# One block of a diffusion backbone: modulation sums ordered behind weight splits, norms by halves, TensorE repeats products while it waits

## The chip, the cores and the metric

One core of a Trainium2 chip runs the whole program. The metric is the device time of one execution in microseconds; below it, "span" is the part of one profiled execution that the trace covers. An instruction queue belongs to each engine: TensorE (PE, with its weight loads as PEld), VectorE (DVE), ScalarE (ACT), GpSimd (POOL), and SyncE (SP), which issues the weight transfers. Each engine works its queue in order and waits on semaphores of the others.

## The reference

For 256 latent tokens and 256 context tokens of width 2048, in float32:

```python
mod_l = jnp.split(silu_c @ w_mod[l] + b_mod[l], 6, axis=-1)
mod_c = jnp.split(silu_cc @ w_mod[l] + b_mod[l], 6, axis=-1)
hl = modulate(rms_norm(xl, norm1_g[l]), mod_l[0], mod_l[1])
hc = modulate(rms_norm(xc, norm1_g[l]), mod_c[0], mod_c[1])
zl = hl @ w_in[l] + b_in[l]               # conv a1, a2 | gelu u, v | q | k | v | three gates
...
y_conv = silu(layer_norm(depthwise_conv31(a1 * sigmoid(a2)))) @ w_conv_out
y_sgu = spatial_gating(gelu(uv)) @ w_sgu_out
y_att = attention_2d(q, k, v, kc, vc) @ w_na_out
x1 = xl + mod_l[2] * ((g_conv * y_conv + g_sgu * y_sgu + g_att * y_att) @ w_o + b_o)
h2 = modulate(rms_norm(x1, norm2_g[l]), mod_l[3], mod_l[4])
x2 = x1 + mod_l[5] * (square(relu(h2 @ w_ff1 + b1)) @ w_ff2 + b2)
out = rms_norm(x2, final_g)
```

The last seven lines are cut to their sense.

## The kernel before, in words

**Products.** Every large product is taken in two parts: an operand is split into a high part that the fast float32 form of TensorE holds exactly, and the rest. A weight piece is 128 rows by 1024 numbers, 512 KB. `Stream` (`fetch`, L71 to L91) brings each in by one transfer on SP into `raw` (eight buffers), ScalarE casts it into `whi` (L90), VectorE subtracts to get `wlo` (L91); `whi` and `wlo` have four buffers each. `mm_w` (L172, L173) takes the weights as stationary operand and writes a "pair", one matmul over 512 and one over 256 columns; `mm_x` (L178 to L180) takes the tokens as stationary operand and writes three matmuls over 512 columns.

**Steps.** The program is one list of steps, `st.steps`. A step is a number of pieces and a function that uses them. `Stream.run` goes through the list and fetches and splits four pieces ahead (`AHEAD`). So the list sets the order on every engine: a split stands on VectorE where its piece is fetched, ahead of the step four pieces earlier. `gate` and `open` hold back pieces until a point in the program, so that their splits don't stand ahead of something urgent.

**Stages of the span.** 0 to 30 us: opening (modulation of the first two rows of tiles by matmuls with 32 columns, norm 1, hidden states h). 30 to 262: k and v of both token sets, in five row blocks, each with its own modulation (`mod_block`, `post`: a reduction `gv` at L335, then transposes of the tokens, `hT` at L348, then h). 263 to 345: q, with attention begun (scores `S` at L532 and L533, maxima `mx` at L534 and L536). To 544: the conv inputs a1 and a2, u and v with GELU. 544 to 956: three branches, n = 0, 1, 2, with their gates. 956 to 1047: w_o. 1047 to 1054: norm 2. To 1768: feed-forward. To 1777: the final norm.

**Modulation, the other four chapters** (`mod_cols`, `modq`). 16 sums, four chapters by four column blocks, in 128 steps of one unsplit 512 KB piece each. VectorE sums up the rows times the condition, two instructions a step (`ga`, L878 and L880). At the end of a sum TensorE takes part: four transposes (`mcol`, L909) or two products with ones (`mrow`, L899). Steps are put between product steps by `MODS_KV`, `MODS_Q`, `MODS_G`: two after every step of the last row blocks once the early modulation is through, one after every q step, two in three steps of the branches n = 1 and 2; the last 32 steps in the feed-forward.

**Conv norm** (`convq`). One entry after each step of branch 1: sums, mean, eight variance steps, `conv_rstd` (L671 to L674, TensorE, VectorE, POOL), `conv_spread` (L699, L700: a diagonal of the row factors times ones, `crs`), eight `conv_out`.

**Norm 2** (`norm2`, `h2_make`). The square sums of both token halves, one reduction, scaling, power on POOL, a spread by two diagonals, then the first four tiles of h2. `x1_transpose` (L1054) turns the residual by tiles: of block 0 to 2 among the products of w_o, of block 3 behind the spread.

## Time and profile before

| | us |
|---|---|
| median of three runs | 1774.8 (1773.57 to 1776.71) |
| the profiled execution | 1779.37 |
| its span | 1777.5 |
| TensorE busy in it | 1729.2 |
| VectorE busy | 1329.9 |
| ScalarE busy | 862.6 |
| mean granted TensorE clock | 0.993 |

A row of a timeline gives the start, the length, the engine, the line of the code, what is written from what, the shapes and how many instructions were joined; in brackets stand the idle time just before it and what ended that. A granted clock of 1.00 is 2.4 GHz, 0.50 is 1.2 GHz. Lengths of matmuls overlap, since they are pipelined; the distance of two starts is what one costs. The page's share of busy time is a mean over stages with different limits, so each place is read in its own stretch.

### The profile page before, as it was taken

The numbers are of one execution on the slowest core, as the hardware profiler recorded it, in microseconds if no ns is written. First come the engines' busy times: TensorE is split into PE (matmuls) and PEld (weight loads), VectorE is DVE, ScalarE is ACT, GpSimd is POOL, SyncE is SP. The second block draws the span as 40 slices with busy tenths as digits, with TensorE's granted clock in tenths as the row PEclk, the third lists the DMA queues.
The fourth block names the chain that finished last, engine by engine and source line by source line (L and its number), as shares of the span: only waits on it lengthen the run. The fifth ranks groups of instructions, "written<-read, shape, count | busy, mean of one in ns | idle before, by whom it ended". The sixth has DMA issues, their size and how long they took to land.

```text
span 1777.5 us, 24004 instructions
## 1 busy us (share of the span) xinstructions
PE 1729.2 (97%) x8727; PEld 1420.9 (80%) x8727; DVE 1329.9 (75%) x2098; ACT 862.6 (49%) x1290; POOL 134.1 (8%) x174
## 2 busy tenths in 40 slices
PE   6999998999999999999999999999999999999997
PEld 3667787788888888778878878888888888888886
DVE  4656999799999977999877569756775576656665
ACT  4433335987555344644444455533543354334443
POOL 2221340111000100200000010000000000000000
PEclk9999999999999999999999999999999999999999
DMA  9887788656766668899995568757876775666552
GB/s 323 274 307 271 257 260 262 162 145 185 221 189 198 181 211 291 285 332 331 320 338 194 188 192 267 239 194 246 257 251 196 241 220 191 204 193 189 186 193 83
DMA packets 266968, 411.86 MB, mean 232 GB/s; under 512 B 13182, under 2 KB 128050, under 8 KB 266850
## 3 DMA queue, kind: packets, MB, share of 16 engines
q1 hardware_dynamic: 259410, 391.21, 68.1%
q0 software_dynamic: 6864, 18.07, 3.8%
q8 instruction: 68, 1.11, 0.3%
q10 hardware_dynamic: 576, 1.05, 0.2%
q14 instruction: 50, 0.41, 0.1%
HBM read 408.18 MB, written 2.10 MB: 231 GB/s over the span
## 4 chain that ended last, share of the span: by engine, by line
PE 70%; issue 10%; DVE 9%; DMA 7%; ACT 2%; SPq 1%; POOL 0%; DVEq 0%; POOLq 0%; ACTq 0%
PE bk L172 17%; PE bk L178 11%; PE bk L180 11%; PE bk L179 11%; PE bk L173 9%; DMA raw<-in_w_mod_dram 6%; DVE wlo L91 4%; DVE ga L880 3%; PE k L172 2%; PE gemv L313 1%; DMA raw<-in_w_in_dram 1%; PE k L173 1%; PE vb L178 1%; PE vb L180 1%; PE vb L179 1%
## 5 line engine op out<-in xcount | busy, mean ns | idle before, releaser
L90 ACT CAST whi<-raw 128x1024 fp32r<-128x1024 f32 x544 | 570.3, 1050 | 612.0 <-PE bk L180 389.6
L91 DVE TENSOR_TENSOR wlo<-raw,whi 128x1024 fp32r<-128x1024 f32 x544 | 668.3, 1231 | 256.5 <-ACT whi L90 254.2
L172 PE MATMUL bk<-h,whi 128*128 128x512 f32 x1536 | 545.5, 399 | 0.2 <-DVE vN L406 0.2
L173 PE MATMUL bk<-h,wlo 128*128 128x256 f32 x1536 | 431.4, 281 | 2.1 <-DVE wlo L91 2.1
L172 PEld LDWEIGHTS bk<-h,whi 128*128 128x128 f32 x1536 | 289.6, 189 | 72.5 <-issue 3.1
L173 PEld LDWEIGHTS bk<-h,wlo 128*128 128x128 f32 x1536 | 291.3, 190 | 4.7 <-DVE wlo L91 3.6
L880 DVE SCALAR_TENSOR_TENSOR ga<-raw,cst,ga 128x512 f32<-128x512 f32 x240 | 185.4, 774 | 65.2 <-DMA raw<-in_w_mod_dram 62.3
L180 PE MATMUL bk<-whi,g 128*128 128x512 f32 x512 | 199.2, 389 | 0.0
L179 PE MATMUL bk<-wlo,g 128*128 128x512 f32 x512 | 199.2, 389 | 0.0
L178 PE MATMUL bk<-whi,g 128*128 128x512 f32 x512 | 199.2, 389 | 0.0
L179 PE MATMUL bk<-wlo,h 128*128 128x512 f32 x448 | 175.2, 391 | 1.9 <-DVE wlo L91 1.9
L178 PE MATMUL bk<-whi,h 128*128 128x512 f32 x448 | 176.2, 393 | 0.0
L180 PE MATMUL bk<-whi,h 128*128 128x512 f32 x448 | 175.1, 391 | 0.0
L180 PEld LDWEIGHTS bk<-whi,g 128*128 128x128 f32 x512 | 96.1, 188 | 20.0
L178 PEld LDWEIGHTS bk<-whi,g 128*128 128x128 f32 x512 | 96.1, 188 | 20.0
L179 PEld LDWEIGHTS bk<-wlo,g 128*128 128x128 f32 x512 | 96.1, 188 | 19.8
L641 DVE SCALAR_TENSOR_TENSOR cT<-uT,wcT,cT 128x244 f32<-128x244 f32 (+14 forms) x240 | 105.0, 479 | 0.5
L179 PEld LDWEIGHTS bk<-wlo,h 128*128 128x128 f32 x448 | 84.6, 189 | 20.4 <-DVE wlo L91 3.2
L180 PEld LDWEIGHTS bk<-whi,h 128*128 128x128 f32 x448 | 84.4, 188 | 17.8
L178 PEld LDWEIGHTS bk<-whi,h 128*128 128x128 f32 x448 | 84.5, 189 | 17.2
L172 PE MATMUL k<-h,whi 128*128 128x512 f32 x256 | 93.9, 408 | 3.2 <-DVE h L358 2.8
L173 PE MATMUL k<-h,wlo 128*128 128x256 f32 x256 | 72.0, 283 | 0.8 <-DVE wlo L91 0.8
(268 smaller groups left out, 2048.4 us busy)
## 6 DMA issues: line engine op xcount, KB each, us to landing
raw<-in_w_ff_dram SPq DMA_DIRECT2D x256, 512.0 KB, 4.1
raw<-in_w_in_dram SPq DMA_DIRECT2D x208, 512.0 KB, 4.5
raw<-in_w_mod_dram SPq DMA_DIRECT2D x192, 512.0 KB, 5.0
raw<-in_w_o_dram SPq DMA_DIRECT2D x32, 512.0 KB, 3.9
raw<-in_w_na_out_dram SPq DMA_DIRECT2D x16, 512.0 KB, 4.2
raw<-in_w_sgu_out_dram SPq DMA_DIRECT2D x16, 512.0 KB, 5.4
raw<-in_w_conv_out_dram SPq DMA_DIRECT2D x16, 512.0 KB, 6.8
bias<-in_na_rpb_dram POOLq DMA_DIRECT2D x16, 192.0 KB, 5.5
```

The costliest lines, as they stand in the source:

```text
L90: nc.scalar.copy(hv, rv)
L91: nc.vector.tensor_tensor(lv, rv, hv.bitcast(F32), ALU.subtract)
L172: PE.matmul(bk, lhsT=hi[:, j, c0 : c0 + P], rhs=xhl, start=start, stop=False)
L173: PE.matmul(bk[:, T:], lhsT=lo[:, j, c0 : c0 + P], rhs=xhl[:, :T], start=False, stop=stop)
L178: PE.matmul(bk, lhsT=xh, rhs=hi, start=start, stop=False)
L179: PE.matmul(bk, lhsT=xh, rhs=lo, start=False, stop=False)
L180: PE.matmul(bk, lhsT=xl, rhs=hi, start=False, stop=stop)
L313: PE.matmul(gb[j][32 * q : 32 * q + 32, :cols], lhsT=cst[:, g], rhs=raw[:, r], start=g < 4, stop=g >= NK - 4, tile_position=(0, 32 * q))
L641: V.scalar_tensor_tensor(a[:, lo:hi], u[:, lo + d : hi + d], wj, a[:, lo:hi], ALU.mult, ALU.add)
L880: V.scalar_tensor_tensor(a[0], raw[:, r], sc, a[0], ALU.mult, ALU.add)
```

## The change

Nothing that is computed changes. The order and the place of work do:

- Opening: seven of the eight pieces of the first modulation block are multiplied a second time into a spare bank (`warm`), and twelve transposes follow the first `hT`; late parameters are loaded in the middle of the block; only one weight split may stand ahead of the first h (`FIRST`).
- A modulation step's sums are issued behind the split of up to two later pieces (`behind`, `LAG`); that sets the order on VectorE's queue and adds no semaphore.
- Modulation steps are placed anew: in the k/v blocks in the last block alone (12 steps, 25 before), 12 of 16 in q, 8, 24 and 20 in the three branches (0, 32 and 32 before), 20 in w_o, 32 in the feed-forward as before. Chapter 4 comes first, 3 third.
- Conv norm: empty entries between its steps, conv outputs at every second step. Residual loads and bias rows (`xb_load`) of three blocks go into branch 2.
- GELU: one VectorE instruction less per tile.
- Norm 2: by token halves, the first while the products of the second run; the third block's `x1_transpose` and 22 transposes (`refill`) behind the last product, 8 more behind the spread; epsilon is a fifth column of the square sums.
- End: the last block is multiplied with the final gain ahead of the row factor.

```diff
 RBUF = 8
-MODS_Q = 1
-MODS_G = 3
+MODS_Q = (0, 1, 2)
+MODS_G = ((2, 8), (0, 2, 4, 6, 8, 10), (0, 3, 5, 8, 10))
+MODS_O = 20
 TAPS_C, TAPS_S, TAPS_G = 1, 3, 3
 AHEAD = 4
+LAG = 2
...
-        nc.vector.tensor_tensor(lv, rv, hv.bitcast(F32), ALU.subtract)
+        self.low[j] = nc.vector.tensor_tensor(lv, rv, hv.bitcast(F32), ALU.subtract)
...
+            self.at = used
             used += len(pieces)
             self.more = lambda used=used: more(used + AHEAD)
             fn(*mine)
+    def behind(self):
+        later = [j for j in self.low if self.at < j <= self.at + LAG]
+        return self.low[max(later)] if later else None
...
+                if bi == 0 and (j, r0) != (1, NK - rt):
+                    for r in range(rt):
+                        q = (r0 + r) % 4
+                        PE.matmul(warm()[32 * q : 32 * q + 32, :cols], lhsT=cst[:, r0 + r], rhs=raw[:, r],
+                                  start=True, stop=True, tile_position=(0, 32 * q))
...
+            if bi == 0 and vs == (0,):
+                for i in range(12):
+                    PE.transpose(warm()[:, :P], gb["ge"][:, :P], ident)
...
-    convq = [lambda i=i: conv_sum(i) for i in (0, 2, 3, 4, 5, 6, 7)] + [conv_mean] + [lambda i=i: conv_var(i) for i in range(8)] + [conv_rstd, conv_spread] + [lambda i=i: conv_out(i) for i in range(8)]
...
+    convq = [lambda i=i: conv_sum(i) for i in (0, 2, 3, 4, 5, 6, 7)] + [idle, conv_mean] + [lambda i=i: conv_var(i) for i in range(8)] + [idle, conv_rstd, idle, idle, conv_spread, idle] + [f for i in range(8) for f in (lambda i=i: conv_out(i), idle)]
...
-        V.tensor_tensor(q, q, z, ALU.mult)
+        S.activation(q, z, AF.Square, scale=GC0 ** 0.5)
+        V.scalar_tensor_tensor(q, q, 1.0, z, ALU.add, ALU.mult)
...
         def mk(r0):
             def fn(raw):
+                split = st.behind()
                 for r in range(2):
...
-                        V.tensor_scalar(a[0], raw[:, r], sc, None, ALU.mult)
-                    else:
-                        V.scalar_tensor_tensor(a[0], raw[:, r], sc, a[0], ALU.mult, ALU.add)
+                    with tc.issue_after(split.ins) if split else nullcontext():
+                        if r0 + r == 0:
+                            V.tensor_scalar(a[0], raw[:, r], sc, None, ALU.mult)
+                        else:
+                            V.scalar_tensor_tensor(a[0], raw[:, r], sc, a[0], ALU.mult, ALU.add)
...
-    for ch in (3, 4, 2, 5):
+    for ch in (4, 2, 3, 5):
...
-    st.steps += early[: ends[0]]
-    st.do(lambda: posts[0]((0,)))
+    st.steps += early[: ends[0] // 2]
     st.do(late_params)
+    st.steps += early[ends[0] // 2 : ends[0]]
+    if FIRST:
+        st.gate(FIRST)
+    def opening():
+        posts[0]((0,))
+        if FIRST:
+            with tc.issue_after(last["h"].ins), tc.issue_after(last["hi"].ins):
+                st.open()
+    st.do(opening)
...
-            if sent >= len(early):
+            if bi == len(BLOCKS) - 1:
                 mod_steps(MODS_KV)
...
-            mod_steps(MODS_Q)
+            mod_steps(i in MODS_Q)
...
+            with tc.issue_after(gload[2, min(cb + 1, 3)].ins):
+                GP.dma_start(xb[cb], x[0][:, cb * 512 : (cb + 1) * 512].rearrange("(t p) n -> p t n", p=P))
...
-                if n and i % MODS_G and len(modq) > 32:
+                if i in MODS_G[n] and len(modq) > 32 + MODS_O:
                     mod_steps(1)
+                if n == 2 and cb and i == XB:
+                    st.do(xb_load(cb - 1))
...
-    while len(modq) > 32:
-        mod_steps(1)
...
-    for cb in range(4):
-        st.do(xb_load(cb))
...
+    st.do(xb_load(3))
...
             st.steps.append(s)
+            if i % 4 and len(modq) > 32:
+                mod_steps(1)
             if cb == 0 and i == 0:
                 st.do(lambda: m_split(3))
-            if cb and i == 1:
+            if cb in (1, 2) and i == 1:
                 st.do(lambda cb=cb: x1_transpose(cb - 1))
...
+    def refill(n):
+        if "fill" not in n2:
+            n2["fill"] = aux("fill")
+        for _ in range(n):
+            PE.transpose(n2["fill"][:, :P], xb[3][:, 0, :P], ident)
+    def norm2(t):
+        if t == 0:
+            n2["rb"] = aux("n2")[:, :T]
+        rs = tp.tile([P, 1], F32, tag="rs", bufs=2, name=nm("n2rs"))
+        V.tensor_reduce(rs, ss2[:, t], axis=AX.X, op=ALU.add)
+        GP.tensor_tensor(rs, rs, mhalf[:, :1], ALU.pow)
+        dg = tp.tile([P, P], F32, tag="dg", bufs=2, name=nm("dg"))
+        V.tensor_scalar(dg, ident, rs, None, ALU.mult)
+        if t:
+            with tc.issue_after(last["mm"].ins):
+                x1_transpose(2, n2["sq"])
+                refill(22)
+        mm = PE.matmul(n2["rb"][:, t * P : (t + 1) * P], lhsT=ones, rhs=dg, start=True, stop=True)
+        h2_make(0, t * P, (t + 1) * P)
+        if t:
+            with tc.issue_after(mm.ins):
+                refill(8)
...
+            V.tensor_tensor(f, xa[kt // 4][:, kt % 4, a:b], n2["rb"][:, a:b], ALU.mult)
+            n2["high"] = S.activation(d[:, a:b], f, AF.Identity, bias=m2B[:, kt : kt + 1])
+            n2["last"] = V.scalar_tensor_tensor(d[:, T + a : T + b], f, m2B[:, kt : kt + 1], d[:, a:b].bitcast(F32), ALU.add, ALU.subtract)
...
+        end = tmp(512, "end")
+        V.tensor_tensor(end, d, fg[3], ALU.mult)
...
-        V.tensor_scalar(rs, rs, 1.0 / D, EPS, ALU.mult, ALU.add)
...
-        with tc.issue_after(n2["last"].ins):
+        with tc.issue_after(n2["last"].ins), tc.issue_after(n2["high"].ins):
...
-    for n in (2, 4, 6):
+    for n in (1, 4, 6):
         st.gate(n)
-    st.do(norm2)
+    st.do(lambda: norm2(0))
+    st.do(lambda: norm2(1))
```

Three places in the order of the queues. The number behind a name is that of its buffer; x2 means twice in a row. First, VectorE at the end of the fourth k/v block, before the change (`ga` modulation sums, `vN` evictions of v, `gv` and `m1B` the modulation of the next block, for which TensorE's transposes `hT` wait):

```order
L880 SCALAR_TENSOR_TENSOR ga_2135<-raw_2075,cst,ga_2135 128x512
L406 TENSOR_TENSOR vN_554<-vN_554,vb_1934 128x512
L880 SCALAR_TENSOR_TENSOR ga_2135<-raw_2075,cst,ga_2135 128x512
L880 SCALAR_TENSOR_TENSOR ga_2135<-raw_2133,cst,ga_2135 128x512
L91 TENSOR_TENSOR wlo_2072<-raw_2069,whi_2071 128x1024
L406 TENSOR_TENSOR vN_563<-vN_563,vb_1948 128x512
L335 TENSOR_REDUCE gv_1982<-gp_1985 128x8
L335 TENSOR_REDUCE gv_1982<-gp_1993 128x8
L338 TENSOR_TENSOR m1B<-gv_1982,pa_104 128x4 x2
```

The same place after it:

```order
L419 TENSOR_TENSOR t_1916<-k_1907,t_1916 128x256
L437 TENSOR_TENSOR vN_436<-vN_436,vb_1928 128x512
L437 TENSOR_TENSOR vN_445<-vN_445,vb_1942 128x512
L437 TENSOR_TENSOR vN_597<-vN_597,vb_1956 128x512
L97 TENSOR_TENSOR wlo_1923<-raw_1920,whi_1922 128x1024
L437 TENSOR_TENSOR vN_606<-vN_606,vb_1970 128x512
L365 TENSOR_REDUCE gv_1984<-gp_1987 128x8
L365 TENSOR_REDUCE gv_1984<-gp_1995 128x8
L369 TENSOR_TENSOR m1B<-gv_1984,pa_104 128x4 x2
```

The sums are gone from here; the reduction `gv` stands behind evictions and one split.

Second, VectorE in branch 2 at the end of its second column block (`m` the merged branches, `wlo` weight splits), before the change:

```order
L847 TENSOR_TENSOR m_6096<-m_6096,th_8349 128x512
L880 SCALAR_TENSOR_TENSOR ga_8579<-raw_8582,cst,ga_8579 128x512
L91 TENSOR_TENSOR wlo_8489<-raw_8486,whi_8488 128x1024
L880 SCALAR_TENSOR_TENSOR ga_8579<-raw_8582,cst,ga_8579 128x512
L880 SCALAR_TENSOR_TENSOR ga_8579<-raw_8604,cst,ga_8579 128x512
L91 TENSOR_TENSOR wlo_8527<-raw_8524,whi_8526 128x1024
L880 SCALAR_TENSOR_TENSOR ga_8579<-raw_8604,cst,ga_8579 128x512
L91 TENSOR_TENSOR wlo_8558<-raw_8555,whi_8557 128x1024
```

The same place after it:

```order
L881 TENSOR_TENSOR m_6073<-m_6073,th_8284 128x512
L97 TENSOR_TENSOR wlo_8379<-raw_8376,whi_8378 128x1024
L917 SCALAR_TENSOR_TENSOR ga_8309<-raw_8330,cst,ga_8309 128x512
L97 TENSOR_TENSOR wlo_8403<-raw_8400,whi_8402 128x1024
L917 SCALAR_TENSOR_TENSOR ga_8309<-raw_8330,cst,ga_8309 128x512
L97 TENSOR_TENSOR wlo_8421<-raw_8418,whi_8420 128x1024
L917 SCALAR_TENSOR_TENSOR ga_8309<-raw_8396,cst,ga_8309 128x512 x2
L97 TENSOR_TENSOR wlo_8469<-raw_8466,whi_8468 128x1024
```

Each sum stood directly ahead of a split; now a sum of `raw_8330` stands behind the splits of `raw_8376` and `raw_8400`, which were fetched later.

Third, TensorE at norm 2 (`bk` the last product of w_o, `n` the spread of the row factors, `x1T` the transposed residual), before the change:

```order
L180 MATMUL bk_9550<-whi_9616,mhl_9068 128x512
L700 MATMUL n_890_9704<-dg_9705,ones_r 128x128
L700 MATMUL n_890_9704<-dg_9708,ones_r 128x128
L1054 MATMUL x1T_9870<-ident,xb_9028 128x128 x4
L1054 MATMUL x1T_9877<-ident,xb_9028 128x128 x4
L172 MATMUL bk_9759<-h_893_9711,whi_9634 128x512
L173 MATMUL bk_9759<-h_893_9711,wlo_9635 128x256
```

The same place after it:

```order
L194 MATMUL bk_9553<-whi_9632,mhl_8973 128x512
L1143 MATMUL n_888_9710<-dg_9714,ones_r 128x128
L1105 MATMUL x1T_9741<-ident,xb_8820 128x128 x4
L1105 MATMUL x1T_9748<-ident,xb_8820 128x128 x4
L1128 MATMUL fill_9755<-ident,xb_8937 128x128 x22
L1143 MATMUL n_888_9710<-dg_9738,ones_r 128x128
L1128 MATMUL fill_9755<-ident,xb_8937 128x128 x8
L1105 MATMUL x1T_9950<-ident,xb_8937 128x128 x4
L1105 MATMUL x1T_9957<-ident,xb_8937 128x128
L184 MATMUL bk_9839<-h_891_9717,whi_9650 128x512
L185 MATMUL bk_9839<-h_891_9717,wlo_9651 128x256
```

One half of the spread stands before the change's fillers and one behind; the third block's transposes and 30 others stand in the gap; of the last block's eight, five come ahead of the first product.

## Rows read from the trace of the kernel before

**Rows 1.** The page: busy time of TensorE, and the group of modulation sums.

```profile
PE 1729.2 (97%) x8727; PEld 1420.9 (80%) x8727; DVE 1329.9 (75%) x2098; ACT 862.6 (49%) x1290; POOL 134.1 (8%) x174
...
L880 DVE SCALAR_TENSOR_TENSOR ga<-raw,cst,ga 128x512 f32<-128x512 f32 x240 | 185.4, 774 | 65.2 <-DMA raw<-in_w_mod_dram 62.3
```

**Rows 2.** Waits of TensorE: what waited, for what; us in total, times, longest.

```profile
PE n L700 <- DVE dg L699: 3.9, 1, 3.9
PE S L532 <- DVE mx L536: 3.6, 2, 3.2
...
PE bk L179 <- DVE wlo L91: 2.5, 4, 1.2
PE bk L173 <- DVE wlo L91: 2.1, 3, 1.5
PE mcol L909 <- DVE ga L880: 2.0, 1, 2.0
PE S L533 <- ACT kl L501: 1.6, 2, 1.3
```

**Rows 3.** Stretches: length, busy PE, PEld, DVE, ACT, POOL, granted clock, DMA, GB/s.

```profile
203.70:207.10 3.40, 3.40 (x10) 2.66 (x9) 3.37 (x10) 1.93 (x4) 0.00 (x0) 0.50 1.05 358
...
560.00:580.00 20.00, 20.00 (x90) 16.54 (x89) 20.00 (x27) 9.25 (x10) 0.91 (x2) 1.00 0.71 214
...
1050.20:1057.10 6.90, 6.02 (x22) 5.30 (x23) 5.33 (x14) 2.62 (x6) 5.18 (x10) 0.51 0.73 219
```

**Rows 4.** Timeline of TensorE in the opening, and one later modulation piece.

```profile
14.96 3.98 PE L313 MATMUL gemv<-raw,cst 128*32 128x256 f32 x32
...
23.90 1.08 PE L313 MATMUL gemv<-raw,cst 128*32 128x256 f32 x8 [0.42 <-DMA raw<-in_w_mod_dram]
...
29.99 0.77 PE L172 MATMUL k<-h,whi 128*128 128x512 f32 x1 [2.79 <-DVE h L358]
...
31.41 0.63 PE L172 MATMUL k<-h,whi 128*128 128x512 f32 x1
...
33.57 0.39 PE L172 MATMUL k<-h,whi 128*128 128x512 f32 x1
...
33.92 0.39 PE L172 MATMUL k<-h,whi 128*128 128x512 f32 x1
...
62.72 1.07 PE L313 MATMUL gemv<-raw,cst 128*32 128x512 f32 x8
```

**Rows 5.** Timeline at the fourth k/v block's end, and VectorE as attention starts.

```profile
199.59 1.53 DVE L880 SCALAR_TENSOR_TENSOR ga<-raw,cst,ga 128x512 f32<-128x512 f32 x2
...
203.01 0.91 PE L348 MATMUL hT<-ident,nat 128*128 128x128 f32 x6 [2.75 <-DVE gv L335]
...
288.62 1.54 DVE L880 SCALAR_TENSOR_TENSOR ga<-raw,cst,ga 128x512 f32<-128x512 f32 x2
```

**Rows 6.** Timeline of TensorE in branch 1, at the conv norm.

```profile
731.08 0.50 PE L671 MATMUL cvar<-ones_r,cq 128*128 128x1 f32 x4
...
735.95 0.73 PE L700 MATMUL crs<-dg,ones_r 128*128 128x128 f32 x4 [1.48 <-DVE dg L699]
```

**Rows 7.** Timeline in branch 2: a sum that waits, and TensorE behind it.

```profile
896.46 0.75 DVE L880 SCALAR_TENSOR_TENSOR ga<-raw,cst,ga 128x512 f32<-128x512 f32 x1 [5.20 <-DMA raw<-in_w_mod_dram]
...
898.41 0.50 PE L179 MATMUL bk<-wlo,h 128*128 128x512 f32 x1 [1.20 <-DVE wlo L91]
```

**Rows 8.** Timeline of w_o's transposes at full clock, then of norm 2.

```profile
984.47 1.04 PE L1054 MATMUL x1T<-ident,xb 128*128 128x128 f32 x8
...
1047.25 0.69 DVE L1043 TENSOR_TENSOR t<-bk,mrow 128x512 f32<-128x512 f32 x1 [0.21 <-PE bk L180]
...
1052.06 1.92 PE L1054 MATMUL x1T<-ident,xb 128*128 128x128 f32 x8
1053.85 0.80 PE L172 MATMUL bk<-h,whi 128*128 128x512 f32 x1
```

**Rows 9.** Timeline of VectorE at the end.

```profile
1770.46 0.15 DVE L1139 TENSOR_SCALAR n3rs<-n3rs 128x1 f32<-128x1 f32 x1
```

More of the change, by code (lines that the diff above doesn't have):

```diff
@@ L1 @@
-from contextlib import ExitStack
+from contextlib import ExitStack, nullcontext
 import concourse.bass as bass
@@ L66, in __init__ @@
         self.n = 0
+        self.at = 0
+        self.low = {}
     def add(self, pieces, fn):
@@ L173, in mm_w @@
         PE.matmul(bk[:, T:], lhsT=lo[:, j, c0 : c0 + P], rhs=xhl[:, :T], start=False, stop=stop)
+    last = {}
     def mm_x(bk, xhl, t, hi, lo, start, stop):
@@ L179, in mm_x @@
         PE.matmul(bk, lhsT=xh, rhs=lo, start=False, stop=False)
-        PE.matmul(bk, lhsT=xl, rhs=hi, start=False, stop=stop)
+        last["mm"] = PE.matmul(bk, lhsT=xl, rhs=hi, start=False, stop=stop)
     w_mod, b_mod, w_in, b_in = w_mod[0], b_mod[0], w_in[0], b_in[0]
@@ L298, in tile_block, with warm @@
         S.copy(vbias[:, i * 512 : (i + 1) * 512], vps)
+    spare = []
+    def warm():
+        if not spare:
+            spare.append(bank("warm"))
+        return spare[0]
     def mod_block(bi):
@@ L820, in tile_block @@
     gbias = {}
+    gload = {}
     def gate_bias(br, cb):
@@ L998, in tile_block, with xb_load, fn @@
     att_steps(100)
+    xb = [None] * 4
+    xa = [None] * 4
+    ss2 = cp.tile([P, 2, 5], F32, name="ss2")
+    GP.memset(ss2[:, :, 4:], EPS)
+    def xb_load(cb):
+        def fn():
+            xb[cb] = unit([P, 2, 512], name="xb")
+            with tc.issue_after(gload[2, min(cb + 1, 3)].ins):
+                GP.dma_start(xb[cb], x[0][:, cb * 512 : (cb + 1) * 512].rearrange("(t p) n -> p t n", p=P))
+            bo = tmp(512, "bo")
+            with tc.issue_after(gload[2, min(cb + 1, 3)].ins):
+                GP.dma_start(bo, bcast(b_o[0][cb * 512 : (cb + 1) * 512], P))
+            V.tensor_tensor(bo, bo, mrow[2, cb], ALU.mult)
+            for t in range(2):
+                V.tensor_tensor(xb[cb][:, t], xb[cb][:, t], bo, ALU.add)
+        return fn
     branches = [(2, w_na_out[0], lambda kt: oT[kt][:, kt % 2]), (1, w_sgu_out[0], lambda kt: sgT[kt][:, kt % 2]),
@@ L1014, in tile_block @@
                     st.do(convq.pop(0))
[L1015 removed]
+                if i in MODS_G[n] and len(modq) > 32 + MODS_O:
                     mod_steps(1)
+                if n == 2 and cb and i == XB:
+                    st.do(xb_load(cb - 1))
         if n == 0:
             taps_steps(1000)
[L1020 to L1037 removed]
+    n2 = {}
     def o_done(cb):
@@ L1044, in fn, with x1_transpose @@
             V.tensor_tensor(d, d, f, ALU.add)
-            S.activation(f, d, AF.Square, accum_out=ss2[:, t, cb : cb + 1])
+            n2["sq"] = S.activation(f, d, AF.Square, scale=D ** -0.5, accum_out=ss2[:, t, cb : cb + 1])
         return fn
-    def x1_transpose(cb):
+    def x1_transpose(cb, after=None):
         xa[cb] = unit([P, 4, T], name="xa")
@@ L1054, in x1_transpose @@
                     PE.transpose(b2[:, i * T + tt * P : i * T + (tt + 1) * P], xb[cb][:, tt, (kk + i) * P : (kk + i + 1) * P], ident)
-            for i in range(2):
-                kt = 4 * cb + kk + i
-                S.activation(xa[cb][:, kk + i], b2[:, i * T : (i + 1) * T], AF.Copy, scale=m2A[:, kt : kt + 1])
-    for cb in range(4):
-        st.do(xb_load(cb))
+            with tc.issue_after(after.ins) if after else nullcontext():
+                for i in range(2):
+                    kt = 4 * cb + kk + i
+                    S.activation(xa[cb][:, kk + i], b2[:, i * T : (i + 1) * T], AF.Copy, scale=m2A[:, kt : kt + 1])
+    st.do(xb_load(3))
     for cb in range(4):
@@ L1091, in tile_block @@
     gT = [None] * NK
     ac = [None] * 4
-    ss3 = cp.tile([P, 2, 4], F32, name="ss3")
+    ss3 = cp.tile([P, 2, 5], F32, name="ss3")
+    GP.memset(ss3[:, :, 4:], EPS)
     NB = DFF // D
```

59 lines of the change are left out of this document (18 added, 41 removed).

## Prediction

> **What bounds the kernel now.** I read the page's table of busy time first. TensorE is busy for 1729.2 of the 1777.5 us of the span, VectorE for 75%, ScalarE for less [rows 1]. So the time is TensorE's, and only two things can be won: the 48 us in which it stands still, and the stretches in which its clock is halved. The waits by engine come second. Before the first weight product nothing can be gained in large sums (inputs arrive). After it, each line names a place and what ended the wait: norm 2 (3.9), the scores at the start of attention (3.6 and 1.6), products that wait for a weight piece's low part (2.5 and 2.1), a column of the modulation (2.0) [rows 2]. Third come stretches with the granted clock: after a standstill of 2 to 4 us the clock stands at 0.50, which is 1.2 GHz, for 3.40 us, and the engine is full all that time [rows 3]. At half speed 3.40 us do the work of 1.70, so each such standstill costs 1.7 us more than its wait. Three are alike, from 203.7, 299.3 and 760.1; the fourth, at norm 2, is 1050.2 to 1057.1. Fourth, the timeline of VectorE at each place shows why it was late: it works its queue in order, and a modulation sum (774 ns [rows 1]) that waits for its transfer holds up the weight split or the score behind it. From 560 to 580 VectorE is full and TensorE waits for nothing [rows 3]: there the engines are level, and VectorE has no room.
>
> **The change part by part.** All against the profiled run of 1779.4 us.
>
> *(a) Opening.* Before, the eight pieces of the first modulation block run at half speed: eight matmuls with 256 columns take 1.08 us, as eight with 512 columns do later [rows 4]; TensorE rests between pieces and again for 2.79 us before the first product at 29.99, and the products still take 0.63 at 31.41 and 0.39 at 33.57, a pair of them then 0.35 from start to start [rows 4]. The records hold no clock there; by the products it changes at 33.06. Half of 33.06 − 29.99 is 1.5 us. The change repeats seven of the eight pieces and adds twelve transposes, so that the engine has no pause; if the clock is full by 29.99, that is 1.5. A copy of parameters and two small scalings leave VectorE's path to the first product: at no less than 0.15 each, as a scaling at the end [rows 9], some 0.5. Together +2.0. Other end: if the clock stays at half, a piece costs 0.86 (two groups of four, 0.43 apart), and 15 times 0.86 from 14.96 ends at 27.9, where the last piece now ends near 24.8: 3.1 later, and 0.4 for transfers that wait for buffers which the repeats hold, −3.5. I take **+2.0**, since the engine would run without a gap from 14.96, and the products from 29.99 on show that a run without a gap brings the clock up.
>
> *(b) End of the k/v blocks.* The reduction that the hidden states need stood behind modulation sums (two in a row at 199.59, three before them); TensorE waited 2.75 [rows 5] and then ran its 3.40 us at half speed [rows 3], 1.70: 4.45 in all. Now modulation stands in the last row block alone, and the order of VectorE has no sum ahead of that reduction in any block but the last. What is late next is the reduction's own chain, some tenths. **+4.2**, ends 0 and 4.5.
>
> *(c) Start of attention.* The waits are 3.2 and 0.4, then 1.3 [rows 2], with one half-speed stretch of 1.70: 6.6. The first maxima stood behind five sums from 288.62 on [rows 5] and two splits, 5 × 0.774 + 2 × 1.23 = 6.3. Now one step less stands in each group of four, and between the evictions and the maxima there is one split and no sum. From the eviction to the freed bank that leaves some 4.7 us of VectorE's work, where the 16 product pairs in between give 16 × 0.35 = 5.6. But VectorE must have caught up by then. **+4.5**, ends −1 and +7.3 (all of it, and the small waits from 333 to 345 too).
>
> *(d) Conv norm.* From the sum of squares on TensorE to its spread lie 731.08 to 735.95, and TensorE waited 1.48 of that [rows 6]; 12 products stood between, 36 stand there now, 8.0 us at 0.22 each (90 instructions in 20.00 [rows 3]), where 4.9 are needed. The column that came too late at 757 (2.0 [rows 2]) and the 1.70 that followed it stood behind the rows of the conv output, which now come at every second step. **+5.0**, ends 1.5 and 5.2.
>
> *(e) Splits behind waiting sums.* At 896 a sum waited 5.20 us for its transfer; the split behind it came late, and TensorE waited 1.20 [rows 7]. All such places are 2.5 and 2.1 [rows 2]. Now a step's sums stand behind the splits of up to two later pieces, so a split waits for its own piece alone. What pays for it: a raw buffer is held for longer, so SP's next transfer starts later, and what is queued behind a waiting sum is now the third split. **+4.2**, ends 0 and 4.6.
>
> *(f) Norm 2.* From the last product's end at 1047.25 to the first product at 1053.85 the chain is eviction 0.69, residual, square, reduction, scaling, power, spread, eight transposes, h [rows 8]. By halves, the first half is worked off while 24 products of the second run, so only one half stands behind the last product; one scaling is gone (0.15 as [rows 9], 0.2 with its gap), and one of two diagonals with its spread product leaves the path (between the power and the transposes at 1052.06; I estimate 0.4): 0.6 earlier. The third block's eight transposes, which stood among the products of the last block, take 1.04 at full clock [rows 8] and delay the products by 0.87 (0.11 from start to start); they go into the gap. Of the fourth block's, three move behind the first products, −0.3. 22 and 8 more transposes fill the gap; if they hold the clock, the half speed from 1053.85 to 1057.1, 3.2 us, costs 1.6 less. In all 0.6 + 0.87 − 0.3 + 1.6 = 2.8, of which I take **+2.6**. Other end: fillers that run at half speed (1.92 for eight [rows 8], so 5.3 for 22 and 7.2 with the eight ahead) end at 1054.4 and hold up the spread by 3, less what is gained: −1.5. Upper end 3.4.
> Here a rule speaks against the change. The trace shows transposes at half speed at 1052.06, but behind a standstill, so it cannot tell what they do to the clock. The Trainium skill, "TensorE: Matmul & The Clock Gate", Part 4 (PE-mode transpose), says that transposes don't count as TensorE activity in the same way. By it the fillers would not keep the clock; by the rows alone I can't say.
>
> *(g) End.* The path loses one scaling (0.15 and its gap, 0.24 from 1770.46 to the power [rows 9]), and the last multiplication loses an operand: **+0.4**, ends 0.2 and 0.5. The GELU loses one VectorE instruction for each of twelve tiles (of at most 0.69 [rows 8], the smaller ones half as wide; estimated at 3.8 in all), which TensorE doesn't wait for.
>
> *(h) New waits.* Sixteen sums of modulation (four chapters by four column blocks), each finished by a product on TensorE, now come later on VectorE against the splits. The order gives the lead, the splits that VectorE has done ahead of the sum beyond the one that TensorE last used: before it was −5 to −1 at thirteen places, and +2 at three; now it is +1 to +3 at all sixteen. Of the three with +2, two waited for nothing and one for 2.0 [rows 2], and no place with a negative lead waited. So a wait at each is from 0 to 2.0, 0 to 32 in all. A split takes 1.23, the products of a piece 2.7 (12 at 0.22) or 2.8 (eight pairs), so VectorE gains on TensorE with every piece. I take **−3**, nearer to the two that were free, since the conv rows that stood ahead of the third are spaced now.
>
> Sum: 2.0 + 4.2 + 4.5 + 5.0 + 4.2 + 2.6 + 0.4 − 3 = 19.9. The profiled run would take 1759.5. The median of the runs is 4.6 under that run, so 1774.8 − 19.9 = **1755** (rounded).
>
> **The rivals.**
> R1, slower: the sixteen finishing products wait. Mechanism: a sum put behind two later splits ends only when those pieces have come and been split; TensorE, in order, stands at the product (place: the branches and the feed-forward). At 2.0 each [rows 2] it is 32 instead of 3: 1774.8 − 22.9 + 32 = 1784. It is slower from 22.9 / 16 = 1.4 us a place. For it: the 2.0 at lead +2. Against it: two other such places were free.
> R2: VectorE is full from 420 to 640, and eight steps with 16 sums go into the first branch there, 16 × 0.774 = 12.4, less 3.8 for the GELU: 8.6 that TensorE may have to pay. 1755 + 8.6 = 1763.5. For it: 20.00 of 20.00 [rows 3]. Against it: TensorE waits for nothing there, so a reserve of unknown size is left.
> R3: the repeats of the opening don't bring the clock up. Four pieces ran in a row from 14.96 to 18.94, and a piece at 23.90 was still at half speed [rows 4], which speaks for it; that the pieces have pauses between them speaks against it. 2.0 becomes −3.5: 1760.5.
> R4: the transposes of norm 2 don't keep the clock. 1.6 and a little more of (f) is missing: 1757. The rule cited in (f) would give this.
> R5: the change doesn't do what it says, as each wait has a second cause just behind it (VectorE's whole load of sums stays the same, and each is only moved): within 0.2% of 1774.8.
>
> **How the numbers follow.** The forecast's case, 1748 to 1759, has 0.40, R4 lying within it at near half of that. R3 alone 0.22, R2 alone 0.14, both together, near 1769, 0.06. R5 0.06, R1 0.08, better than 1748 0.04. A difference under 0.2% (3.5 us) can't be told from none by a measurement of this kernel. Faster by more: 0.40 + 0.22 + 0.14 + 0.06 + 0.04 = 0.86; within 0.06; slower 0.08. For 8 in 10 the range reaches from below the forecast's case to R2 and R3 together: 1746 to 1771.
>
> **What would show it.** (a): pairs at 0.35 from the first k product on, which stands before 29.5; R3: 0.64, and a later one. (b), (c): no wait for gv or for mx over 0.5 us, and no clock of 0.50 near 204 or 299. (d): no wait of crs; mcol under 0.5. (e): the lines of waits for wlo under 1 us. (f): granted clock 1.0 from 1048 to 1057, less the shift; R4: 0.5 at the first feed-forward products. (h), R1: lines mcol and mrow in the waits, their sum and count. R2: products waiting for wlo or banks between 420 and 680, with VectorE full. The forecast is wrong if TensorE's waits after the opening are still over 15 us in all, or a new line stands at their head.

## The result, and the profile after

| | before | after |
|---|---|---|
| median of four runs, us | 1775.76 (1773.57 to 1780.57) | 1758.07 (1755.90 to 1758.92) |
| ratio, 95% interval | | 0.9875 (0.9856 to 0.9895) |
| profiled execution, us | 1779.37 | 1758.92 |
| its span | 1777.5 | 1757.1 |

The forecast was 1755, in a range of 1746 to 1771. By the medians the change is worth 17.7 us, by the two spans 20.4, since the profiled execution of before was one of its longer ones. Steps are weighed below by the spans, as the sum was.

The page of after, against [rows 1]: busy time of the engines; the share of the chain that ended last, by engine; and the groups of weight splits and of modulation sums (busy us, mean ns, then idle time just before them).

```profile
PE 1729.2 (98%) x8825; PEld 1423.0 (81%) x8825; DVE 1331.4 (76%) x2094; ACT 866.7 (49%) x1294; POOL 130.9 (7%) x177
...
PE 79%; ACT 1%; issue 1%; DVE 1%; POOL 0%; POOLq 0%; DVEq 0%; ACTq 0%
...
L97 DVE TENSOR_TENSOR wlo<-raw,whi 128x1024 fp32r<-128x1024 f32 x544 | 669.3, 1232 | 289.2 <-ACT whi L96 282.4
...
L917 DVE SCALAR_TENSOR_TENSOR ga<-raw,cst,ga 128x512 f32<-128x512 f32 x240 | 183.6, 765 | 2.3
```

TensorE's busy time is the same 1729.2 us to a tenth, although 98 instructions were added; what was saved is time in which it stood still. The last row says how. VectorE stood idle for 65.2 us just ahead of modulation sums, 62.3 of it for their transfers [rows 1]; now it is 2.3. The sums take as long as before, but when one comes to the head of the queue its piece has landed.

The waits of TensorE, against [rows 2] (us in total, times, longest):

```profile
...
PE k L184 <- DVE h L389: 2.2, 2, 2.0
PE k L184 <- DVE t L419: 1.0, 1, 1.0
PE hT L379 <- ACT nat L275: 0.9, 1, 0.9
PE S L564 <- ACT kl L532: 0.9, 1, 0.9
PE mcol L946 <- DVE ga L917: 0.8, 1, 0.8
...
PE mrow L936 <- DVE ah L934: 0.5, 1, 0.5
```

The lines for n, for mx, for wlo and for crs are gone, and nothing new over 1.0 has come. Where the time went is read from the start of the first product of each stage in the two traces:

| start of | before | after | shift |
|---|---|---|---|
| first k product | 29.99 | 30.19 | +0.2 |
| first q product | 262.86 | 260.72 | −2.1 |
| first product with attention's output (branch 0) | 565.47 | 556.74 | −8.7 |
| first of branch 1's second part | 700.21 | 691.43 | −8.8 |
| first of branch 2's second part | 839.70 | 826.21 | −13.5 |
| first of w_o | 956.35 | 939.11 | −17.2 |
| last of w_o | 1046.83 | 1030.13 | −16.7 |
| first of the feed-forward | 1053.85 | 1035.85 | −18.0 |
| last product | 1767.64 | 1747.40 | −20.2 |
| end of the span | 1777.5 | 1757.1 | −20.4 |

The opening of after, against [rows 4], and its granted clock (length, busy PE, PEld, DVE, ACT, POOL, clock, DMA, GB/s):

```profile
18.48 1.08 PE L335 MATMUL gemv<-raw,cst 128*32 128x256 f32 x8
...
24.85 0.61 PE L335 MATMUL gemv<-raw,cst 128*32 128x256 f32 x8
...
30.19 0.47 PE L184 MATMUL k<-h,whi 128*128 128x512 f32 x1 [2.05 <-DVE h L389]
...
31.49 0.63 PE L184 MATMUL k<-h,whi 128*128 128x512 f32 x1
```

```profile
31.08:34.49 3.41, 3.41 (x13) 2.83 (x12) 2.66 (x5) 2.03 (x5) 0.00 (x0) 0.50 1.05 382
```

The pieces run twice as fast from about 21 on, so the clock came up with the repeats, which before it hadn't (that it needs them isn't shown, see a1). But TensorE rested 2.05 us before the first product, the clock fell at 31.08 after all, and the first product came 0.2 later than before.

Norm 2 of after, against [rows 8]:

```profile
1031.45 2.56 PE L1128 MATMUL fill<-ident,xb 128*128 128x128 f32 x22
...
1034.06 0.49 PE L1143 MATMUL n<-dg,ones_r 128*128 128x128 f32 x2
1034.39 1.04 PE L1128 MATMUL fill<-ident,xb 128*128 128x128 f32 x8
...
1035.26 0.71 PE L1105 MATMUL x1T<-ident,xb 128*128 128x128 f32 x5
...
1035.85 0.50 PE L184 MATMUL bk<-h,whi 128*128 128x512 f32 x1
```

The fillers run at full speed, 0.11 us each, and the first products do too.

### The profile page after: what moved, and what is told of

Read it like the earlier page. It is cut to its first block, busy times and chain, and to the rows that moved or that the text cites. A ratio compares the mean times of both kernels' runs of the same rounds, so it can differ in the third digit from the quotient of the medians.

```text
span 1757.1 us, 24169 instructions
## 1 busy us (share of the span) xinstructions
PE 1729.2 (98%) x8825; PEld 1423.0 (81%) x8825; DVE 1331.4 (76%) x2094; ACT 866.7 (49%) x1294; POOL 130.9 (7%) x177
## 4 chain that ended last, share of the span: by engine, by line
PE 79%; ACT 1%; issue 1%; DVE 1%; POOL 0%; POOLq 0%; DVEq 0%; ACTq 0%
PE bk L184 18%; PE bk L194 16%; PE bk L193 16%; PE bk L192 16%; PE bk L185 9%; PE o L597 1%; PE pT L586 1%; ACT whi L96 0%; PE mrow L936 0%; PE S L563 0%; PE S L564 0%; PE mix L842 0%; PE mT L891 0%; PE mcol L946 0%; ACT s L570 0%
## 5 line engine op out<-in xcount | busy, mean ns | idle before, releaser
L672 DVE SCALAR_TENSOR_TENSOR cT<-uT,wcT,cT 128x248 f32<-128x248 f32 (+14 forms) x240 | 104.6, 481 | 0.5
L193 PEld LDWEIGHTS bk<-wlo,h 128*128 128x128 f32 x448 | 84.1, 188 | 17.2
```

The costliest lines, as they stand in the source:

```text
L193: PE.matmul(bk, lhsT=xh, rhs=lo, start=False, stop=False)
L672: V.scalar_tensor_tensor(a[:, lo:hi], u[:, lo + d : hi + d], wj, a[:, lo:hi], ALU.mult, ALU.add)
```

## The experiments

The kernels a0 to a3, b1 to b4 and c1 to c4 each share a chip, and runs of the kernel before, against which their ratios stand. A difference of medians of 1 to 2 us isn't resolved by these intervals (about ±0.0016, or 2.8 us), so smaller effects are read from the traces.

**a0: the changed kernel again.**

> The changed kernel again, as the mark for the other runs of this chip. All theories: near 1758 us, 0.9875 of the kernel before; first k product near 30.2, granted clock 0.50 from 31.1 to 34.5 and nowhere else before the end.

1757.05 us, 0.9856 (0.9840 to 0.9873). The opening was not the same: TensorE rested longer, and yet the clock didn't fall.

```profile
30.65 0.47 PE L184 MATMUL k<-h,whi 128*128 128x512 f32 x1 [3.29 <-DVE h L389]
```

```profile
31.10:34.40 3.30, 3.30 (x21) 2.92 (x20) 3.14 (x6) 2.34 (x6) 0.00 (x0) 1.00 1.05 382
```

So the same program with a rest of 2.05 lost the clock and with one of 3.29 kept it. Eight of the traced kernels have this same opening (after, a0, b1 to b4, c2, c4): three lost the clock there (after, b1 and c2, rests of 2.0 to 2.6), five kept it (rests of 1.5 to 3.3). What the opening is worth can't be read from one trace.

**a1: no repeats in the opening.**

```diff
-                if bi == 0 and (j, r0) != (1, NK - rt):
+                if False:
...
-                for i in range(12):
+                for i in range(0):
```

> The changed kernel without the seven repeats and the twelve transposes of the opening. Theory (the repeats bring the clock up, but TensorE rests 2.05 us before the first product and loses it again at 31.1; and they hold raw buffers, so that the first weight piece lands 1.2 us later): first product near 29.5, half clock until about 33 as in the kernel before, time 0.2 to 0.9 us less than the changed kernel. Rival (the repeats earn their time): first product not earlier, time 1 to 2 us more.

1755.79 us, 0.9849 (0.9835 to 0.9864), the lowest median of its group, and 1.3 under a0, which isn't resolved. In the trace the first product stands at 29.22, 1.0 earlier than in after, although the clock was low from 26.65 to 33.48, and the first q product at 257.71, 3.0 earlier. The clock had come up without any repeat, since here the first five pieces follow on one another from 15.43 on; the sixth already runs at full speed, 0.64 for eight matmuls where [rows 4] had 1.08:

```profile
20.99 0.64 PE L335 MATMUL gemv<-raw,cst 128*32 128x256 f32 x8 [0.31 <-DMA raw<-in_w_mod_dram]
```

So what the repeats give is less than the theory's clock. TensorE's wait for the tokens at 44 (`hT` for `nat`, 0.9 in after) is gone. That agrees with the theory: without the repeats' hold on raw buffers the first cast of a weight piece starts at 25.5 instead of 26.5. That the later transfers are late for the same reason isn't shown by it: in c3 below, where no buffer is held either, the wait for the tokens stays.

**a2: 30 transposes in place of 12.**

```diff
-                for i in range(12):
+                for i in range(30):
```

> The changed kernel with 30 transposes in place of 12 behind the first hT, so that TensorE runs until about 30.1. Theory (the rest before the first product takes the clock away): no clock of 0.50 near 31, first product at the same place, 1.7 us less than the changed kernel. Rival (transposes don't count as work for the clock): 0.50 for 3.4 us around 30 all the same, no difference.

1757.77 us, 0.9861 (0.9846 to 0.9876). The clock was 1.00 up to the end, the first product at 30.17, the first q product 1.5 earlier than in after: as the theory said, by place and size. Against a0, which kept its clock by chance, there is nothing left of it. That transposes alone hold the clock is seen here:

```profile
27.00:30.00 3.00, 3.00 (x30) 3.00 (x29) 2.86 (x9) 2.91 (x5) 0.00 (x0) 1.00 1.05 383
31.10:34.40 3.30, 3.30 (x21) 2.83 (x20) 3.09 (x7) 2.78 (x8) 0.00 (x0) 1.00 1.05 383
```

**a3: 24 transposes, and no repeat of the first piece.**

```diff
-                if bi == 0 and (j, r0) != (1, NK - rt):
+                if bi == 0 and (j, r0) not in ((0, 0), (1, NK - rt)):
...
-                for i in range(12):
+                for i in range(24):
```

> The changed kernel with 24 transposes, and without the repeat of the first piece, so that its buffer is free 0.9 us earlier for the first weight piece. Theory (first weight transfer waits for the buffer that the repeat holds): first weight cast 0.8 us earlier, first product near 29.5, clock 1.00 throughout, 2.0 to 2.5 us less than the changed kernel. Rival (the transfers' rate sets the first weight piece, not the buffer): first product at 30.2, and 1.7 less at most; or the clock falls because the transposes end before the product.

1756.86 us, 0.9853 (0.9838 to 0.9868). The first product came at 29.03, 1.2 earlier, with the clock at 1.00: one buffer held by one repeat was what delayed it, since a2, with more transposes and all repeats, had 30.17. The span is 2.0 under that of after, though only 0.1 under that of a0; the first weights came earlier, but the wait for the tokens stayed, 0.9.

**b1: no fillers at norm 2.**

```diff
-                refill(22)
+                refill(0)
...
-                refill(8)
+                refill(0)
```

> The changed kernel without the 22 and 8 transposes that only fill the gap at norm 2. Theory (they hold the clock): TensorE rests some 2.5 us, the clock is 0.50 for 3.4 us at the first feed-forward products, and the run takes 1.5 to 1.9 us more than the changed kernel; the first product comes no earlier. Rival (transposes don't count as work for the clock, the gap by halves is short enough by itself): clock 1.00 or the same, difference under 0.3 us.

1759.30 us, 0.9877 (0.9862 to 0.9891). The same two stretches, of after and then of this kernel:

```profile
1031.40:1034.00 2.60, 2.60 (x24) 2.37 (x22) 2.22 (x10) 2.33 (x8) 0.87 (x2) 1.00 0.16 58
1036.80:1040.10 3.30, 3.30 (x21) 2.83 (x20) 3.30 (x5) 3.13 (x5) 1.71 (x4) 1.00 0.89 282
```

```profile
1031.40:1034.00 2.60, 0.80 (x6) 0.43 (x5) 2.22 (x9) 2.40 (x8) 1.04 (x2) 1.00 0.08 27
1036.80:1040.10 3.30, 3.30 (x12) 2.82 (x12) 3.30 (x5) 3.30 (x6) 1.53 (x3) 0.50 0.98 292
```

Without the transposes the clock falls, with them it doesn't: 12 instructions against 21 in the same 3.3 us. So the fillers do hold it: all eleven traced kernels with them have 1.00 through norm 2, and the three without (before, b1, c1) fall to 0.50 there. Counted from the last product of w_o, this kernel's first product is 0.3 later than that of after, and the products just behind its half-speed stretch 1.8 later, so the clock costs 1.5, as expected. At the end of the span 0.75 is left: 0.3 comes back as three transposes that this kernel has done earlier, and between 1061 and 1116 the pairs run closer with no wait in the records, which gives 0.9 (see the last section); later changes of that kind nearly cancel.

**b2: the new places without the order.**

```diff
-                split = st.behind()
+                split = None
```

> The changed kernel without the order of modulation sums behind later splits; the places of the steps stay. Theory (a split behind a waiting sum is what TensorE waits for): waits for wlo of 2 to 4 us in all come back in the branches and the feed-forward, and 2.5 to 4.5 us more than the changed kernel. Rival (the new places alone cured it): within 1 us.

1786.45 us, 1.0024 (1.0010 to 1.0038): slower than the kernel before, by 4.0 in the medians of this chip, and 28.7 over the changed one by the spans. Both expectations were far too small. TensorE's waits, and VectorE's group of sums:

```profile
PE bk L193 <- DVE wlo L97: 7.4, 6, 4.0
...
PE pT L586 <- ACT s L574: 6.3, 2, 5.3
PE mT L891 <- DVE m L881: 4.9, 1, 4.9
PE bk L185 <- DVE wlo L97: 3.8, 3, 2.3
```

```profile
L917 DVE SCALAR_TENSOR_TENSOR ga<-raw,cst,ga 128x512 f32<-128x512 f32 x240 | 185.4, 772 | 105.5 <-DMA raw<-in_w_mod_dram 103.2
```

These lines are 22.4 us, and the clock fell at 299.34, 835.23 and 964.94 (for 6.83, 3.41 and 3.41 us at half, 6.8 lost): together 29.2, near the 28.7 of the spans, though the account is a rough one (after lost 1.7 to the clock in its opening, this kernel didn't). The sums also move forward in VectorE's queue when nothing holds them: 18 of the 128 steps are summed before the first q product, 13 in after. So the places of this kernel aren't quite the new ones. One of the places, where a sum waits 6.54 for its transfer and two splits stand behind it:

```profile
831.61 1.54 DVE L917 SCALAR_TENSOR_TENSOR ga<-raw,cst,ga 128x512 f32<-128x512 f32 x2 [6.54 <-DMA raw<-in_w_mod_dram]
833.07 2.35 DVE L97 TENSOR_TENSOR wlo<-raw,whi 128x1024 fp32r<-128x1024 f32 x2
```

**b3: conv rows close again.** The list `convq` as in the kernel before, without its empty entries.

```diff
-    convq = [lambda i=i: conv_sum(i) for i in (0, 2, 3, 4, 5, 6, 7)] + [idle, conv_mean] + [lambda i=i: conv_var(i) for i in range(8)] + [idle, conv_rstd, idle, idle, conv_spread, idle] + [f for i in range(8) for f in (lambda i=i: conv_out(i), idle)]
+    convq = [lambda i=i: conv_sum(i) for i in (0, 2, 3, 4, 5, 6, 7)] + [conv_mean] + [lambda i=i: conv_var(i) for i in range(8)] + [conv_rstd, conv_spread] + [lambda i=i: conv_out(i) for i in range(8)]
```

> The changed kernel with the conv norm's entries back in close order, as before the change. Theory: the wait of crs (1.5) comes back, conv outputs pile up ahead of the sums so that a mcol or mrow waits again (2.0), and the clock halves once (1.7): 3 to 5.2 us more. Rival (the late mcol came from the sums' own place, which the change moved): crs alone, 1.5 to 1.8 more.

1758.86 us, 0.9875 (0.9860 to 0.9890). From the first branch to branch 2's second part it loses 0.95 us in a wait of mrow for ScalarE (0.9), and nothing more. The wait of crs doesn't come back, and the clock doesn't fall. Its chain, to be held against [rows 6]:

```profile
722.37 0.50 PE L702 MATMUL cvar<-ones_r,cq 128*128 128x1 f32 x4
...
722.90 0.16 DVE L704 TENSOR_SCALAR conv_rs<-cvar 128x2 f32<-128x2 f32 x1 [0.70 <-PE cvar L702]
...
725.59 0.61 PE L734 MATMUL crs<-dg,ones_r 128*128 128x128 f32 x4
```

VectorE waits for TensorE here, where before a split, two sums and another split stood ahead of the scaling. The chain takes 3.2 us instead of 4.9, and 12 products cover it. Spacing was not the cure.

**b4: the old places with the new order.**

```diff
-            if bi == len(BLOCKS) - 1:
+            if sent >= len(early):
...
-            mod_steps(i in MODS_Q)
+            mod_steps(1)
...
-                if i in MODS_G[n] and len(modq) > 32 + MODS_O:
+                if n and i % 3 and len(modq) > 32:
```

> The changed kernel with the modulation steps where they were before (two after each step of the last k/v blocks once the early ones are through, one after every q step, two in three in branches 1 and 2, none in w_o), but the order behind later splits kept. Theory (places, not the order, cured the k/v blocks' end and the start of attention): TensorE waits 2 to 3 us for gv and 2 to 4 for mx or S, one or two stretches at 0.50: 5 to 10 us more than the changed kernel. Rival (the order behind splits alone does it): under 2 us more.

1762.69 us, 0.9898 (0.9883 to 0.9913). The time is at the theory's lower bound (5.6 over the median of a0, on another chip, and 3.2 over after by the spans), but its places are not. Neither gv (0.2) nor mx waits; what came instead is this (2.4 of the mcol in the last k/v block), and a fall of the clock at 236.81:

```profile
PE mcol L946 <- DVE ga L917: 3.1, 2, 2.4
...
PE S L564 <- ACT kl L532: 2.0, 2, 1.1
```

**c1: the kernel before with the order alone.** Nothing else of the change is in it.

```diff
+LAG = 2
...
+    def behind(self):
+        later = [j for j in self.low if self.at < j <= self.at + LAG]
+        return self.low[max(later)] if later else None
...
+                split = st.behind()
...
+                    with tc.issue_after(split.ins) if split else nullcontext():
```

> The kernel before with one part of the change alone: modulation sums ordered behind the splits of up to two later pieces. Since the run without that order lost 29 us and the run with the old places only 5, theory A (the order carries most of the gain by itself) expects 10 to 14 us less than the kernel before, no wait for wlo over 0.5 us, no wait of crs over 0.5 and at most two stretches at 0.50 before the end. Theory B (order and places need each other; either alone gives little) expects 0 to 5 us less, with waits for gv or mx left.

1769.04 us, 0.9937 (0.9919 to 0.9954): 11.4 us under the kernel before on that chip, 9.7 by the spans. That is theory A by its number, and half of what the whole change gives. Waits for mx and crs have gone, those for wlo too but for 0.8 and 0.7 in the k/v blocks, and sums wait for transfers no more; the finishing products now stand first, with norm 2 untouched behind them:

```profile
PE mcol L920 <- DVE ga L891: 5.5, 4, 2.5
PE n L708 <- DVE dg L707: 3.9, 1, 3.9
```

```profile
L891 DVE SCALAR_TENSOR_TENSOR ga<-raw,cst,ga 128x512 f32<-128x512 f32 x240 | 184.6, 769 | 2.5
```

**c2, c4: one and four later splits.**

```diff
-LAG = 2
+LAG = 1
```

> The changed kernel with the order behind one later split in place of two. Theory A (one split ahead of a waiting sum is not enough cover, since the transfer of a modulation piece can be 5 us late): 5 to 20 us more than the changed kernel, with waits for wlo. Theory B (any later split is enough): within 1.5 us.

> The changed kernel with the order behind up to four later splits. Theory (the finishing products of the sixteen sums are next in line: each split more puts a sum up to 2.8 us later): waits of mcol and mrow grow from 1.3 to 8 us or more and raw buffers are held longer, 5 to 20 us more. Rival (sums have room to be later still): within 2 us.

One: 1755.40 us, 0.9860 (0.9842 to 0.9878), idle time ahead of sums 3.1. Four: 1759.36, 0.9882 (0.9864 to 0.9900), the waits of mcol and mrow 1.1 and 0.8. Neither is told apart from the changed kernel; theory A fell in the first, and the theory in the second. What counts is that a sum is not ahead of the next splits at all. How far behind matters little for the waits of mcol and mrow (1.6 in all with one split, 1.9 with four). The two are 4.0 apart by the medians, with no overlap of their runs, and 2.7 by the spans; some 2 us of c2's lead are closer pairs in the feed-forward (see the last section), and that the number of splits makes the rest isn't shown.

**c3: the identity in place of the repeats.**

```diff
-                        PE.matmul(warm()[32 * q : 32 * q + 32, :cols], lhsT=cst[:, r0 + r], rhs=raw[:, r],
-                                  start=True, stop=True, tile_position=(0, 32 * q))
+                    for _ in range(4):
+                        PE.transpose(warm()[:, :P], ident, ident)
...
-                for i in range(12):
+                for i in range(24):
```

> The changed kernel with the repeats of the opening replaced by four transposes of the identity after each of the seven pieces, and 24 in place of 12 at the end: TensorE is kept running, but no raw buffer is held. Theory (the repeats' cost is the buffers that they hold; what they give is the clock): first product near 29.2 as without repeats, clock 1.00 up to the end, no wait of hT for the tokens at 44; span 1751 to 1753, 2 to 4 us less than the changed kernel. Rival (the transfers of the opening are paced by their rate, and buffers matter little): first product near 30, 1755 or more.

1756.73 us, 0.9870 (0.9849 to 0.9892); span 1753.9, 3.2 under after. The first product came at 29.13 with the clock at 1.00 up to the end, as expected, but the wait for the tokens at 44 stayed (1.0). By the spans it is the best that keeps the clock, by the medians no better than the changed kernel. a1, a3, c2 and c3 each have a lower median than a0 and after; none is resolved from them.

**The parts by place.** Products are matched one by one with those of after. Each row says by how many us a kernel falls behind after in a stretch (−: gains on it):

| stretch (times of after) | before | order alone (c1) | old places, order (b4) | new places, no order (b2) |
|---|---|---|---|---|
| to 160 | −1.8 | −0.9 | −2.0 | −1.3 |
| 160 to the first q product, 261 | 3.9 | 5.7 | 5.6 | 2.7 |
| to 342, start of attention | 7.7 | 1.8 | 1.3 | 7.1 |
| to branch 0, 557 | −1.1 | −1.1 | 0.1 | 0.0 |
| branches, to 939 | 8.5 | 3.3 | 1.6 | 9.9 |
| w_o, to 1030 | −0.5 | −0.6 | −1.4 | 6.7 |
| from there to the end | 3.7 | 2.6 | −1.9 | 3.6 |
| sum (unrounded) | 20.4 | 10.7 | 3.2 | 28.7 |

These are single executions, and two of the changed kernel (after, a0) end 1.9 apart by their spans. The start of attention and the branches go with the order, whatever the places. The k/v blocks don't: with the order at the old places they are slower than before, and only both together cure them.

## Why the prediction was right, point by point

The sum, 19.9, was near 17.7 by the medians and 20.4 by the spans. Its terms were right in part only, and the nearness is partly luck: the opening came out 3.8 below its term, the start of attention 3.2 above.

**(a) Opening, +2.0: wrong.** Measured −0.2 at the first product and −1.8 by the products at 160; the trace of after has the half clock behind the first product, as before. The step that failed is "the engine would run without a gap from 14.96": it does so up to 28.1, and then rests for the weights' split and for h. What stood in its place is a term that I had put at the lower end only, transfers waiting for buffers that the repeats hold. a1 and a3 show it as 1.0 to 1.2 at the first product; at the first q product a1 is 3.0 earlier and a3, which also kept its clock, 2.1. R3 (the clock doesn't come up) was wrong too: it comes up, even without repeats (a1), and may be lost again, or not (a0).

**(b) End of the k/v blocks, +4.2: size right, cause half told.** A block's products moved from 1.2 late to 3.7 early at that place, 4.9. I gave it to the places ("modulation stands in the last row block alone"). They don't do it without the order: b2 has them, and TensorE waits 1.8 for gv there and 1.1 for hf behind it. Nor does the order without the places: in b4 gv waits 0.2 only, but a wait of 2.4 for mcol and a half clock come 30 us later, and the stretch loses 5.6, more than the 3.9 of the kernel before. And 1.4 is given back in the last block, which now has two steps after each product step: a wait of 1.0 for a k eviction, behind a split of 1.76 us.

**(c) Start of attention, +4.5: too small.** From the first q product to 351 it is 7.7, above the 6.6 that I had added up, and over the upper end of 7.3. I had discounted for VectorE not catching up; it does, as it no longer waits for transfers. Here the order does most of it: c1 gains 7.5 by 302 and keeps 5.9 of it (it starts q 2.6 behind the kernel before), b4 loses 1.3 of the 7.7 and b2 7.1.

**(d) Conv norm, +5.0: size right, mechanism wrong.** The branch shows 4.7. The step "12 products stood between, 36 stand there now" is not what did it: b3 puts 12 back and loses 0.95, and c1, with the old list, has no wait of crs either. The 4.9 us that the chain took before were no property of the chain; 1.7 of them were VectorE's queue, with sums in it.

**(e) Splits behind sums, +4.2: right.** The waits for wlo are gone, and the shifts at the two places are 2.6 (867 to 910) and 1.8 (1308 to 1344). The mechanism was right, and its reach was under-rated: the same cure makes most of (c), the wait in (d), and with the places (b). Read as one, the row of 65.2 us of VectorE's idle time ahead of sums should have been the first row of the argument; I quoted it for its 774 ns alone.

**(f) Norm 2, +2.6: a little less.** From w_o's last product to the products just behind the stretch that had run at half speed 2.7, of which 2.1 are left by the second half of the feed-forward's first block; w_o itself grew by 0.55, with modulation steps in it and the transposes gone. The clock's part is 1.5 by b1 at its place, near the 1.6. R4 is refuted: transposes hold the clock here, as b1 and a2 show. The Trainium skill, "TensorE: Matmul & The Clock Gate", Part 4 (PE-mode transpose), says that they don't count in the same way; for float32 transposes that follow on products in this kernel the measurement decides against it (1.00 with them, 0.50 without). Whether transposes alone would raise a low clock no run shows.

**(g) End, +0.4:** 0.2 by the spans (−20.24 at the last product, −20.40 at the end), at the lower bound.

**(h) New waits, −3:** −1.3, one mcol of 0.8 and one mrow of 0.5 in sixteen places. R1 is real at the old places (5.5 in c1, 3.1 in b4, with a fall of the clock in each) and is what the new places are good for. R2 (VectorE full from 420 to 640): the shift is −8.74 at 502 and −8.77 at 701, so the eight steps cost nothing there. VectorE was busy for 118.9 of the branch's 134 us before and for 124.2 after: the row of 560 to 580 was not the whole branch.

## What to carry to other kernels

Look first at the idle time ahead of each group of instructions of an engine that works in order, and put work that nobody waits for behind work that somebody waits for, by an order edge that costs no semaphore. An order and the places of the work are one choice: without the order the rest of the change made this kernel 4 us slower by the medians (8 by the spans), the order alone made it 11 faster (10 by the spans), and the new places took another 3 off the ordered kernel by the spans. A filler that reads a buffer holds it: the first product came 1.1 earlier with fillers that read a constant (c3).

## What the runs showed of the hardware that I had not expected

**Two rhythms of the same products.** Pairs of `mm_w` at full clock, with no wait in the records, go in one of two steady patterns, which last for tens of us and then change. After, then b1, at the same time:

```profile
1070.18 0.40 PE L184 MATMUL bk<-h,whi 128*128 128x512 f32 x1
...
1070.55 0.40 PE L184 MATMUL bk<-h,whi 128*128 128x512 f32 x1
...
1070.89 0.40 PE L184 MATMUL bk<-h,whi 128*128 128x512 f32 x1
```

```profile
1070.05 0.39 PE L184 MATMUL bk<-h,whi 128*128 128x512 f32 x1
...
1070.39 0.40 PE L184 MATMUL bk<-h,whi 128*128 128x512 f32 x1
...
1070.74 0.39 PE L184 MATMUL bk<-h,whi 128*128 128x512 f32 x1
```

From 1070 to 1082 the pairs of after are on average 353 ns apart (steps of 360, 350 and 350), those of b1 347. Over 1536 such pairs that is up to 10 us. It gave b1 back 0.9 us by 1118, cost after 1.1 against before between 441 and 502, and is of the size by which runs of one kernel differ. What sets it stays open.

**VectorE beside GpSimd.** In the last k/v block a split takes 1.76 us while GpSimd adds up k; in an earlier block, where less of the add is left when the split starts, it takes 1.44:

```profile
227.36 1.18 POOL L420 TENSOR_TENSOR kT<-kT,t 128x256 f32<-128x256 f32 x1 [1.50 <-DVE t L419]
...
227.86 1.76 DVE L97 TENSOR_TENSOR wlo<-raw,whi 128x1024 fp32r<-128x1024 f32 x1
```

```profile
108.16 0.74 POOL L420 TENSOR_TENSOR kT<-kT,t 128x256 f32<-128x256 f32 x1 [25.23 <-DVE t L419]
...
108.54 1.44 DVE L97 TENSOR_TENSOR wlo<-raw,whi 128x1024 fp32r<-128x1024 f32 x1 [0.52 <-ACT whi L96]
```

Of the 544 splits of after, the 521 that overlap no arithmetic or copy of GpSimd take 1.24 us at most, and all 14 over 1.3 us overlap one. In the nine cases where only an add of GpSimd overlaps and had begun first, the split takes 1.22 us and the overlap less 0.14: 0.68 of overlap gives 1.76, 0.36 gives 1.44. So a split makes next to no progress while such an add runs. The Trainium skill, "SBUF — State Buffer", Terms, says that the two engines arbitrate for one pair of ports, and that the loser blocks for the whole instruction; the trace agrees but for the 0.14. No kernel was run without GpSimd's adds. It is part of what (b) gave back.
